# Four of sixteen gates computed by Strassen's scheme inside the values' stage, and queries repeated by transfers

## The chip, the cores and the metric

The kernel runs on one core of one Trainium2 chip. The metric is the device time of one execution in microseconds, the median of several runs. The core has a matrix engine (TensorE, PE in the profile, its weight loads PEld), three other engines that compute (VectorE or DVE, ScalarE or ACT, GpSimd or POOL) and a synchronisation engine (SyncE or SP) that issues most DMA transfers. ACT and POOL issue transfers too, each on a queue of its own. An engine works its instructions off in order.

## The reference

One layer of a decoder trunk on 1024 tokens with 1024 features, in float32:

```python
h    = rms_norm(x, pre_mix_g)
proj = h @ w_in                      # q, k, v of attention A; q, k, v of attention B; 2 x 1024 gates
qa, ka, va, qb, kb, vb, gates = split(proj)
oa   = diff_attention(rope(qa), rope(ka), va, lam)    # 4 heads, two softmaxes of 64-wide queries, v 128 wide
ya   = (rms_norm(oa) * 0.8) @ w_a_out
ob   = merge of three dilated window attentions (4 heads each, 128 wide)
yb   = ob @ w_b_out
g_a, g_b = split(sigmoid(gates))
x    = x + rms_norm((g_a * ya + g_b * yb) @ w_mix_out)
x    = x + rms_norm(conv-gated MLP of rms_norm(x))
```

Attention A is causal; for each of its 4 heads it makes two score matrices (64 features each), takes the softmax of each and subtracts the second, scaled by lambda, from the first. The gates are 2048 columns of the projection, 16 blocks of 128, used only after both attentions.

## The kernel before

A float32 product is made of three matmuls: an operand is split into a high half, rounded to the format that TensorE reads at full speed (`F32R`), and a low half, the rest; `mm3` (L153 to L157) issues high*high, low*high and high*low into one accumulation. `split` (L148) makes the high half by a copy on ACT (L149) and the low half by a subtraction on DVE (L146). A unit of work of TensorE is thus a 128x128 weight and 512 moving columns, three times over.

The work before the convolution stage comes in this order:

1. *The values' stage.* h, not yet divided by its norm, stands in SBUF as `xh` and `xl` (128 features x 8 chunks x 1024 tokens). The 2048 value columns of A and B are computed by Strassen's scheme of seven products (p1 to p7) in two rounds i = 0, 1 of 1024 columns each: feature halves and token halves on the one side (`b11`, `b12`, `b21`, `b22` and the sums `t2`, `t3`, `t4`; `b12` holds the sum T1 until it is made again near the end), column halves on the other. `steps_v` is the hand-written list of 56 steps (product, round, chunk k); a step is 12 matmuls. `fetch_v` loads its weights, one or two 128x512 blocks, 8 to 10 steps ahead into a ring of buffers; `ready_v` adds or subtracts them on DVE (p5, p6, p7, p3) and splits them, 4 steps ahead; `step_v` issues the matmuls, and at the fourth chunk `take_v` moves the sums out of PSUM into quarters of the result. `put_v` scales a quarter by 1/norm and stores it to DRAM from POOL's queue; `STORE_AT` says before which step the first round's quarters are stored. Between steps the list also places the norms (`NORM_AT`), the angles, sines and tables of the rotation (`ANGLES_AT`, `SINES_AT`, `TABLES_AT`) and, from `TABLES_AT + 4` on, more load buffers.
2. *A first gate, and head 0's queries and keys.* `gate(i)` is a projection (`proj_t`): 2 token halves x 8 chunks x 3 matmuls, its weights loaded and split in two pieces by `load_unit`; `put_gate` scales it (L250) and stores it to `gt_d` from ACT's queue.
3. *The first attention (A).* Each of the 4 heads has 8 jobs `attend_a` (128 queries each); PE is given fill between them by `interleave`, in the order of the letters in `A_FILLS`: g is a gate, p the next head's queries and keys (`proj_a`), v, w, x, V fetch or split values, P is the first projection of attention B. Work that follows a job is put off by `later`.
4. *Attention B* with its own fills, and the last three gates (`B_GATES`).

The order in each engine's queue is made by a planner that simulates the traced program with costs of its own; blocks under `high_priority` are moved ahead, and `behind_marks` pins an instruction behind another.

In `proj_a` the rotated queries of one score matrix go into a tile of 128 partitions, high half in one half of the partitions and low half in the other (`q0`, `q1`); the keys' high half is written twice, into both halves of the partitions (`k0`, `k1`, at L756 and L757), and so is their low half (`l0`, `l1`, at L760). One matmul against k and one against l (L783, L784) then give all four terms of the product of 64 features.

PSUM has eight banks: `acc` 3, `pt` 2, `ps_s` 2, `ps_o` 1. In the values' stage a product uses four: p1, p6, p7, p4 three of `acc` and `ps_o`, p2, p5, p3 two of `ps_s` and two of `pt`.

Of the kernel before, what the change touches and what calls it, by code (L numbers as in the profile page):

```python
# [24 lines left out]
P = 128  # L25
# [24 lines left out]
START_GATES, A_FILLS, B_GATES = 1, ("gpgg", "gpvgg", "wgpgg", "xgPVgg"), 3  # L50
# [4 lines left out]
XT_BUFS, NORM_AT, ANGLES_AT, SINES_AT, TABLES_AT, STORE_AT = 6, 14, 25, 33, 34, {35: 0, 36: 3, 39: 2, 41: 1}  # L55
# [32 lines left out]
def trunk(ctx: ExitStack, tc: tile.TileContext, a, out):  # L88
# [111 lines left out]
    def halves():  # L200
        return [slice(i * 512, (i + 1) * 512) for i in range(2)]
# [139 lines left out]
    def f32(v):  # L341
        return v.bitcast(F32)
# [4 lines left out]
    def slot(name, shape=(P, S), dt=F32R):  # L347

        return slots.tile(list(shape), dt, tag="slot", name=name, bufs=SLOTS)
# [111 lines left out]
    with ExitStack() as st_y:  # L461
# [6 lines left out]
        def turns(pattern, *ps):  # L468

            ks = [iter(range(4)) for _ in ps]  # L470
            return [(ps[c], 1, next(ks[c])) for c in pattern]

        steps_v += [("p1", 1, k) for k in range(4)] + turns((0, 0, 1, 0, 1, 0, 1, 1), "p5", "p6")
# [15 lines left out]

        def fetch_v(n):  # L490
            p, i, k = steps_v[n]
            which = {"p1": ((0, 0),), "p2": ((0, 1),), "p5": ((1, 0), (1, 1)), "p6": ((0, 0),), "p7": ((0, 0), (1, 0)),
                     "p4": ((1, 1),), "p3": ((0, 1),)}[p]
            got_v[n] = [load_raw(a["w_v"][j * 4 + k][:, (2 * i + c) * 512 : (2 * i + c + 1) * 512], next(tags), parts=1 if n else 2)
                        for c, j in which]
# [59 lines left out]

        def step_v(n):
            p, i, k = steps_v[n]
            x = xs_of[p]
# [73 lines left out]
        for n in range(8, len(steps_v)):  # L632
# [23 lines left out]
            if n == TABLES_AT:  # L656
                turn_norms()
            if k == 0 and (p, i) in places_y:
                q, name, pool = places_y[p, i]
                quarter[q, i] = new_y(name, pool)  # L660
# [81 lines left out]
    def proj_a(h, res):  # L742
        q0, q1, k0, k1, l0, l1 = (slot(n) for n in ("q0", "q1", "k0", "k1", "l0", "l1"))
        res += [q0, q1, k0, k1, l0, l1]

        def put_q(half, sl, ps):
            t = rotated(ps, cos_a, sin_a, sl, 32)
            nc.scalar.activation(q0[u, sl], t[u], AF.Copy)
            nc.scalar.activation(q1[v, sl], t[v], AF.Copy)
            nc.vector.tensor_tensor(q0[v, sl], t[u], q0[u, sl].bitcast(F32), op=ALU.subtract)  # L750
            nc.vector.tensor_tensor(q1[u, sl], t[v], q1[v, sl].bitcast(F32), op=ALU.subtract)

        def put_k(half, sl, ps):
            t = rotated(ps, cos_a, sin_a, sl, 32)
            for part, kk in ((u, k0), (v, k1)):
                nc.scalar.activation(kk[u, sl], t[part], AF.Copy)  # L756
                nc.scalar.activation(kk[v, sl], t[part], AF.Copy)  # L757
            for part, kk, ll in ((u, k0, l0), (v, k1, l1)):
                for to in (u, v):
                    nc.vector.tensor_tensor(ll[to, sl], t[part], kk[part, sl].bitcast(F32), op=ALU.subtract)  # L760

        yield from proj_t(QA + h * P, put_q)
        yield from proj_t(KA + h * P, put_k)

    def attend_a(h, i, ops, vs, out_sb, pair):

        q0, q1, k0, k1, l0, l1 = ops
# [10 lines left out]
        for c, (qq, kk, ll) in enumerate(((q0, k0, l0), (q1, k1, l1))):  # L778
            s_sb = wk_a.tile([P, S], F32, tag="s", name="s", bufs=4)
            sc.append(s_sb)  # L780
            for n, (c0, c1) in enumerate(chunks):
                ps = psum(F32, ps_s, "s")[:, : c1 - c0]
                nc.tensor.matmul(ps, qq[:, qs], kk[:, c0:c1], start=True, stop=False)  # L783
                nc.tensor.matmul(ps, qq[:, qs], ll[:, c0:c1], start=False, stop=True)  # L784
# [86 lines left out]
    free_gates = list(range(2 * KC))  # L871
# [929 lines left out]
```

## Time and profile before

| | |
|---|---|
| median of three runs | 1688.93 us (1688.74 to 1690.08) |
| the profiled execution | 1693.0 us, its span 1691.1 us |
| granted TensorE clock, mean | 0.997 |
| PE, DVE, ACT, POOL busy | 1672.0, 1318.6, 923.9, 161.9 us |
| values' stage, first gate, head 0's projections | about 5 to 161, 161 to 172, 172 to 194 us |
| first attention with its fills | within 192 to 545 us |
| moved by DMA | 237.40 MB, 140 GB/s |

The profile is of one execution. Busy time of PE counts each matmul to its modelled end, and matmuls overlap, so a busy PE is not yet a PE without gaps; who waited for whom is a view of its own. In a row of a group stand line, engine, operation, what it writes and reads, shape and count, then busy us and mean ns of one, then the engine's idle time just before and what ended it. In a view of stages stand the stage's bounds and length, the busy us (and instructions) of PE, PEld, DVE, ACT and POOL, the granted clock, the busy share of the DMA engines and GB/s.

### The profile page before, as it was taken

What the parts mean: (1) busy time and instruction counts of PE and PEld (TensorE: products, weight loads), DVE (VectorE), ACT (ScalarE), POOL (GpSimd) and SP (SyncE); (2) the same over time, 40 slices, a digit from 0 to 9 for tenths busy, and PEclk for the clock granted to TensorE, in tenths of its full rate; (3) what the DMA queues carried; (4) which work ended last, traced back from release to release, by engine and by line L of the source; (5) the groups of instructions that cost most, each with busy time, mean ns of one, the idle gap of its engine ahead of it and who ended that gap; (6) DMA issues with size and microseconds to landing.
All of it is one profiled execution on the core that took longest, in us unless ns stands there. A gap on an engine that the chain in (4) does not pass through costs nothing. (4 is left out here: it accounts for less than half of the span.)

```text
span 1691.1 us, 22909 instructions
## 1 busy us (share of the span) xinstructions
PE 1672.0 (99%) x7878; PEld 1395.7 (83%) x7878; DVE 1318.6 (78%) x2446; ACT 923.9 (55%) x1723; POOL 161.9 (10%) x251
## 2 busy tenths in 40 slices
PE   9999999999999999999999999999999999999997
PEld 7888888888888888888878888888888888878886
DVE  8794686877777777788866865988888778689978
ACT  7643575655554777667653533565555455255463
POOL 0031000000000000010123400022211121000000
PEclk9999999999999999999999999999999999999999
DMA  8777311214112122333676632267655655296524
GB/s 273 228 248 245 98 59 61 88 57 121 48 63 81 55 72 77 107 120 119 208 257 215 203 112 87 51 162 171 163 132 133 154 134 128 98 338 214 197 88 149
DMA packets 115973, 237.40 MB, mean 140 GB/s; under 512 B 14272, under 2 KB 23424, under 8 KB 115856
## 3 DMA queue, kind: packets, MB, share of 16 engines
q1 hardware_dynamic: 89296, 171.28, 30.4%
q0 software_dynamic: 21808, 56.26, 14.2%
q10 hardware_dynamic: 4752, 8.39, 1.3%
q8 instruction: 62, 1.02, 0.2%
q14 instruction: 55, 0.45, 0.1%
HBM read 177.54 MB, written 47.86 MB: 133 GB/s over the span
## 5 line engine op out<-in xcount | busy, mean ns | idle before, releaser
L157 PE MATMUL acc<-xl,whi 128*128 128x512 f32 x768 | 303.2, 395 | 0.0
L155 PE MATMUL acc<-xh,whi 128*128 128x512 f32 x768 | 302.1, 393 | 0.0
L156 PE MATMUL acc<-xh,wlo 128*128 128x512 f32 x768 | 301.9, 393 | 0.0
L149 ACT ACTIVATE whi<-raw 128x512 fp32r<-128x512 f32 (+1 forms) x249 | 153.9, 626 | 162.6 <-PE acc L157 94.2
L146 DVE TENSOR_TENSOR wlo<-raw,whi 128x512 fp32r<-128x512 f32 (+1 forms) x249 | 171.9, 698 | 27.8 <-ACT whi L149 23.5
L156 PEld LDWEIGHTS acc<-xh,wlo 128*128 128x128 f32 x768 | 144.6, 188 | 28.2
L157 PEld LDWEIGHTS acc<-xl,whi 128*128 128x128 f32 x768 | 144.6, 188 | 28.0
L155 PEld LDWEIGHTS acc<-xh,whi 128*128 128x128 f32 x768 | 144.7, 188 | 27.5
L155 PE MATMUL acc<-mh,whi 128*128 128x512 f32 x384 | 149.7, 390 | 1.4 <-ACT u L1446 1.1
L156 PE MATMUL acc<-mh,wlo 128*128 128x512 f32 x384 | 149.4, 389 | 0.0
L157 PE MATMUL acc<-ml,whi 128*128 128x512 f32 x384 | 149.1, 389 | 0.0
L700 ACT ACTIVATE t<-acc 64x512 f32<-64x512 f32 (+1 forms) x160 | 94.6, 591 | 60.1 <-PE acc L157 58.2
L149 ACT ACTIVATE whi<-s 128x512 fp32r<-128x512 f32 x80 | 49.8, 627 | 90.8 <-PE acc L157 68.7
L1442 DVE TENSOR_TENSOR u<-acc,u 128x512 f32<-128x512 f32 x100 | 68.4, 685 | 28.4 <-PE acc L157 28.2
L701 DVE TENSOR_TENSOR t<-acc,cos 128x512 f32<-128x512 f32 x64 | 44.2, 690 | 59.4 <-ACT t L700 58.9
L155 PEld LDWEIGHTS acc<-mh,whi 128*128 128x128 f32 x384 | 72.1, 188 | 17.4 <-ACT u L1446 2.0
L157 PEld LDWEIGHTS acc<-ml,whi 128*128 128x128 f32 x384 | 72.1, 188 | 15.0
L156 PEld LDWEIGHTS acc<-mh,wlo 128*128 128x128 f32 x384 | 72.1, 188 | 14.7
L1619 PE MATMUL acc<-whi,wlo 128*128 128x512 f32 x216 | 76.0, 390 | 0.0
L1618 PE MATMUL acc<-whi 128*128 128x512 f32 x216 | 74.9, 390 | 0.3 <-ACT whi L149 0.3
L1620 PE MATMUL acc<-wlo,whi 128*128 128x512 f32 x216 | 71.6, 390 | 0.0
L793 ACT ACTIVATE s<-s,mx 128x896 f32<-128x896 f32 (+7 forms) x64 | 49.3, 771 | 35.1 <-DVE mx L786 18.8
(403 smaller groups left out, 4033.9 us busy)
## 6 DMA issues: line engine op xcount, KB each, us to landing
raw<-in_w_in SPq DMA_DIRECT2D x96, 256.0 KB, 2.9
raw<-in_w_v SPq DMA_DIRECT2D x71, 256.0 KB, 5.0
raw<-in_w_up SPq DMA_DIRECT2D x68, 256.0 KB, 3.5
raw<-c_d SPq DMA_DIRECT2D x48, 256.0 KB, 3.7
c_d<-c SPq DMA_DIRECT2D x22, 512.0 KB, 3.9
s<-in_w_up POOLq DMA_DIRECT2D x40, 256.0 KB, 4.1
s<-s POOLq DMA_DIRECT2D x40, 256.0 KB, 3.9
raw<-in_w_down SPq DMA_DIRECT2D x37, 256.0 KB, 3.6
```

What stands on the lines that cost most here:

```text
L146: eng.tensor_tensor(lo, src, hi.bitcast(F32), op=ALU.subtract)
L149: copy = nc.scalar.activation(hi, src, AF.Copy)
L155: nc.tensor.matmul(o, sh, mh, start=first, stop=False, skip_group_check=on)
L156: nc.tensor.matmul(o, sl, mh, start=False, stop=False, skip_group_check=on)
L157: nc.tensor.matmul(o, sh, ml, start=False, stop=last, skip_group_check=on)
L700: nc.scalar.activation(t1[dst], ps[src], AF.Copy)
L701: nc.vector.tensor_tensor(t2, ps, cos[:, sl], op=ALU.mult)
L793: exp = nc.scalar.activation(sc[c][:, :w], sc[c][:, :w], AF.Exp, bias=mx[:, c, 0:1], scale=-1.0, accum_out=den[:, c : c + 1])
L1442: nc.vector.tensor_tensor(to, made(p), x, op=ALU.add)
L1618: nc.tensor.matmul(banks[m], gh[:, tk], wh, start=f == 0, stop=False)
L1619: nc.tensor.matmul(banks[m], gl[:, tk], wh, start=False, stop=False)
L1620: nc.tensor.matmul(banks[m], gh[:, tk], wl, start=False, stop=f == NH - 1)
```

## The change

Four gates, 12 to 15 (`PAIRS` = 2 pairs), are no longer computed by `gate`; `A_FILLS` has two letters g for each head where there were three. They become 14 new steps of the values' stage, in place behind the fourth chunk of p1 in round 1, at step 36: for each of p2, p1, p5, p6, p7, p4, p3 one step for either pair, again of 12 matmuls (4 chunks, one 512-column output). Here the gates' weights are stationary and h moves. A pair has a bank of `pt` and one of `ps_s`, accumulated across products as the values' are, while the values' p1 rests in its four banks. `fetch_v` loads the blocks from `w_in`; `ready_v` is unchanged. `take_gate` moves a product out, scales it by 1/norm and stores it from POOL's queue. The results stand in the tiles of the values' first and third quarters ("a0", "b3") between their uses; the stores of the first round's quarters are moved to steps 32, 37, 42 and 46.

In `proj_a` the keys' tile now holds the high half in one half of the partitions and the low half in the other, each written once, and the queries are repeated instead: high halves (`a0`, `a1`) and low halves (`b0`, `b1`) are computed for one half of the partitions and copied to the other by four transfers a head from POOL's queue, behind the second token half. The number and shape of the matmuls of the scores stay.

```diff
-START_GATES, A_FILLS, B_GATES = 1, ("gpgg", "gpvgg", "wgpgg", "xgPVgg"), 3
+PAIRS, START_GATES, A_FILLS, B_GATES = 2, 1, ("gpg", "gpvg", "wgpg", "xgPVg"), 3
-... TABLES_AT, STORE_AT = ..., 34, {35: 0, 36: 3, 39: 2, 41: 1}
+... TABLES_AT, STORE_AT = ..., 34, {32: 0, 37: 3, 42: 2, 46: 1}
-        steps_v += [("p1", 1, k) for k in range(4)] + turns((0, 0, 1, 0, 1, 0, 1, 1), "p5", "p6")
+        steps_v += [("p1", 1, k) for k in range(4)]
+        steps_v += [(p, "gate", x) for p in ("p2", "p1", "p5", "p6", "p7", "p4", "p3") for x in range(PAIRS)]
+        steps_v += turns((0, 0, 1, 0, 1, 0, 1, 1), "p5", "p6")
...
+            if i == "gate":
+                srcs = [w_in[where[GT + gate_of(k, c) * P]][:, j * 512 : (j + 1) * 512] for c, j in which]
...
+        def take_gate(p, n, use):
+            def put(q):
+                sl = halves()[q % 2]
+                y = gate_y[n][q]
+                tt(y, use if p == "p4" else y, rstd_row[:, sl], ALU.mult)
+                nc.gpsimd.dma_start(gt_d[gate_of(n, q // 2)][:, sl], y)
+            y = gate_y[n]
+            if p in ("p2", "p6", "p7"):
+                nc.scalar.activation(y[{"p2": 0, "p6": 1, "p7": 3}[p]], use, AF.Copy)
+            if p == "p1":
+                tt(y[0], use, y[0], ALU.add)
+                put(0)
+            if p == "p7":
+                tt(y[3], banks[n, False], y[3], ALU.add)
+                put(3)
+            if p == "p4":
+                put(2)
+            if p == "p3":
+                tt(y[1], use, y[1], ALU.add)
+                put(1)
+        def step_gate(p, n, wh, wl):
+            left = p in ("p1", "p6", "p7", "p4")
+            if p in ("p1", "p2"):
+                banks[n, left] = psum(F32, pt, "pt") if left else psum(F32, ps_s, "s")
+            x, use = xs_of[p], banks[n, left]
+            for k in range(4):
+                c = slice(k * P, (k + 1) * P)
+                mm3(use, wh[:, c], wl[:, c], x[0][:, k], x[1][:, k], k == 0 and p in ("p1", "p2", "p5"), k == 3, p in ("p6", "p7", "p4", "p3"))
+            with tc.high_priority(offset=80):
+                take_gate(p, n, use)
...
+            if (p, i, k) == ("p2", "gate", 0):
+                ya, yb = new_y("a0"), new_y("b3", yw)
+                gate_y.update({x: {0: ya[x], 1: ya[2 + x], 3: yb[x], 2: yb[2 + x]} for x in range(PAIRS)})
...
         def put_q(half, sl, ps):
             t = rotated(ps, cos_a, sin_a, sl, 32)
-            nc.scalar.activation(q0[u, sl], t[u], AF.Copy)
-            nc.scalar.activation(q1[v, sl], t[v], AF.Copy)
-            nc.vector.tensor_tensor(q0[v, sl], t[u], q0[u, sl].bitcast(F32), op=ALU.subtract)
-            nc.vector.tensor_tensor(q1[u, sl], t[v], q1[v, sl].bitcast(F32), op=ALU.subtract)
+            for part, hi in ((u, a0), (v, a1)):
+                nc.scalar.activation(hi[part, sl], t[part], AF.Copy)
+            for part, hi, lo in ((u, a0, b0), (v, a1, b1)):
+                nc.vector.tensor_tensor(lo[part, sl], t[part], f32(hi[part, sl]), op=ALU.subtract)
+            if half:
+                for x, from_, to in ((a0, u, v), (a1, v, u), (b0, u, v), (b1, v, u)):
+                    side(x[to], x[from_])
         def put_k(half, sl, ps):
             t = rotated(ps, cos_a, sin_a, sl, 32)
             for part, kk in ((u, k0), (v, k1)):
-                nc.scalar.activation(kk[u, sl], t[part], AF.Copy)
-                nc.scalar.activation(kk[v, sl], t[part], AF.Copy)
-            for part, kk, ll in ((u, k0, l0), (v, k1, l1)):
-                for to in (u, v):
-                    nc.vector.tensor_tensor(ll[to, sl], t[part], kk[part, sl].bitcast(F32), op=ALU.subtract)
+                nc.scalar.activation(kk[part, sl], t[part], AF.Copy)
+            for part, to, kk in ((u, v, k0), (v, u, k1)):
+                nc.vector.tensor_tensor(kk[to, sl], t[part], f32(kk[part, sl]), op=ALU.subtract)
...
-    free_gates = list(range(2 * KC))
+    free_gates = list(range(2 * (KC - PAIRS)))
```

More of the change, by code (lines that the diff above doesn't have):

```diff
@@ L49 @@
 MIX_UNITS = {3: (0,), 4: (1,), 5: (2, 4), 6: (5,), 7: (6, 3, 7)}
-START_GATES, A_FILLS, B_GATES = 1, ("gpgg", "gpvgg", "wgpgg", "xgPVgg"), 3
+PAIRS, START_GATES, A_FILLS, B_GATES = 2, 1, ("gpg", "gpvg", "wgpg", "xgPVg"), 3
 SLOTS = 18
 LEFT_PAD = 48
-XT_BUFS, NORM_AT, ANGLES_AT, SINES_AT, TABLES_AT, STORE_AT = 6, 14, 25, 33, 34, {35: 0, 36: 3, 39: 2, 41: 1}
+XT_BUFS, NORM_AT, ANGLES_AT, SINES_AT, TABLES_AT, STORE_AT = 6, 14, 25, 33, 34, {32: 0, 37: 3, 42: 2, 46: 1}
 K_FIRST = (4, 0, 5, 1, 6, 2, 7, 3)
@@ L488, in new_y, with gate_of @@
             return [(pool or yv).tile([P, 512], F32, tag=f"y{name}{m}", name="yv") for m in range(4)]
+        def gate_of(x, c):
+            return 2 * (KC - PAIRS + x) + c
         def fetch_v(n):
@@ L493, in fetch_v @@
                      "p4": ((1, 1),), "p3": ((0, 1),)}[p]
-            got_v[n] = [load_raw(a["w_v"][j * 4 + k][:, (2 * i + c) * 512 : (2 * i + c + 1) * 512], next(tags), parts=1 if n else 2)
-                        for c, j in which]
+            if i == "gate":
+                srcs = [w_in[where[GT + gate_of(k, c) * P]][:, j * 512 : (j + 1) * 512] for c, j in which]
+            else:
+                srcs = [a["w_v"][j * 4 + k][:, (2 * i + c) * 512 : (2 * i + c + 1) * 512] for c, j in which]
+            got_v[n] = [load_raw(src, next(tags), parts=1 if n else 2) for src in srcs]
         def ready_v(n, w=512):
@@ L554, in trunk @@
         banks = {}
+        gate_y = {}
+        def take_gate(p, n, use):
[28 more added lines that the diff above has]
+                take_gate(p, n, use)
         def step_v(n):
             p, i, k = steps_v[n]
+            if i == "gate":
+                step_gate(p, k, *ready.pop(n))
+                return
             x = xs_of[p]
@@ L742, in proj_a @@
     def proj_a(h, res):
-        q0, q1, k0, k1, l0, l1 = (slot(n) for n in ("q0", "q1", "k0", "k1", "l0", "l1"))
-        res += [q0, q1, k0, k1, l0, l1]
+        a0, a1, b0, b1, k0, k1 = (slot(n) for n in ("a0", "a1", "b0", "b1", "k0", "k1"))
+        res += [a0, a1, b0, b1, k0, k1]
         def put_q(half, sl, ps):
             t = rotated(ps, cos_a, sin_a, sl, 32)
-            nc.scalar.activation(q0[u, sl], t[u], AF.Copy)
-            nc.scalar.activation(q1[v, sl], t[v], AF.Copy)
-            nc.vector.tensor_tensor(q0[v, sl], t[u], q0[u, sl].bitcast(F32), op=ALU.subtract)
-            nc.vector.tensor_tensor(q1[u, sl], t[v], q1[v, sl].bitcast(F32), op=ALU.subtract)
+            for part, hi in ((u, a0), (v, a1)):
[5 more added lines that the diff above has]
+                    side(x[to], x[from_])
         def put_k(half, sl, ps):
@@ L765, in attend_a @@
     def attend_a(h, i, ops, vs, out_sb, pair):
-        q0, q1, k0, k1, l0, l1 = ops
+        a0, a1, b0, b1, k0, k1 = ops
         scale = QK ** -0.5
@@ L777, in attend_a @@
         sc = []
-        for c, (qq, kk, ll) in enumerate(((q0, k0, l0), (q1, k1, l1))):
+        for c, (qh, ql, kk) in enumerate(((a0, b0, k0), (a1, b1, k1))):
             s_sb = wk_a.tile([P, S], F32, tag="s", name="s", bufs=4)
@@ L782, in attend_a @@
                 ps = psum(F32, ps_s, "s")[:, : c1 - c0]
-                nc.tensor.matmul(ps, qq[:, qs], kk[:, c0:c1], start=True, stop=False)
-                nc.tensor.matmul(ps, qq[:, qs], ll[:, c0:c1], start=False, stop=True)
+                nc.tensor.matmul(ps, qh[:, qs], kk[:, c0:c1], start=True, stop=False)
+                nc.tensor.matmul(ps, ql[:, qs], kk[:, c0:c1], start=False, stop=True)
                 mask = mask_a[:, 512 - (c1 - c0) :] if c1 == w else mask_a[:, 0:1].to_broadcast([P, 512])
```

## The prediction

> **What bounds the kernel now.** I read the page's busy shares and slices first, then the waits of TensorE (PE), then its timeline, then each engine's busy time by stage.
>
> ```profile
> span 1691.1 us, 22909 instructions
> PE 1672.0 (99%) x7878; PEld 1395.7 (83%) x7878; DVE 1318.6 (78%) x2446; ACT 923.9 (55%) x1723; POOL 161.9 (10%) x251
> PEclk9999999999999999999999999999999999999999
> ```
>
> TensorE is busy for 99% of the span, at full clock nearly everywhere. A busy PE could still hide waits, because the ends of its matmuls are modelled; so the view of PE's waits comes next (what waited, for whom: total us, times, longest).
>
> ```profile
> PE acc L155 <- ACT xh L387: 2.3, 2, 1.4
> PE pt L713 <- ACT rows L1050: 1.4, 1, 1.4
> PE o L725 <- DVE osb L1027: 1.2, 1, 1.2
> PE acc L155 <- DVE ya L1210: 0.8, 1, 0.8
> ```
>
> No wait is longer than 1.4 us, and none of the helpers that feed the projections or the first attention (the splits at L146 and L149, the scores' L786) heads a long one. TensorE's own work is the bound, so a matmul less is time won, at the spacing of matmuls and not at their length. The timeline of PE shows both (start, duration):
>
> ```profile
> 150.44 0.39 PE L155 MATMUL acc<-whi,t4h 128*128 128x512 f32 x1
> ...
> 152.93 0.39 PE L157 MATMUL o<-wlo,t4h 128*128 128x512 f32 x1
> ```
>
> Between these two rows stand ten more matmuls: eleven steps in 2.49 us, 0.226 us each, although each is drawn 0.39 us long.
>
> **The change, part by part.**
>
> *Matmuls.* A gate is a projection of 128 columns: two halves of the tokens, eight chunks, three matmuls each, 48 in all and 10.9 us at 0.226. Four gates are 192 matmuls (43.5 us), all in the first attention now. Strassen's scheme takes two gates as a 2x2 problem with seven products of 4 chunks and three matmuls: 7 x 12 x 2 pairs = 168 matmuls (38.0 us), put behind the values' step 35. PE gains 24 x 0.226 = **5.4 us**. The scores keep their number and shapes of matmuls, so the repeated queries give PE nothing.
>
> The rows above give 0.226 us for a 512-column matmul with a weight load of its own. The Trainium skill, "TensorE: Matmul & The Clock Gate", section Back-to-back issue gap, states that a sustained stream of such pairs with N=512 comes to about 131 ns each. By that figure the 24 matmuls would be worth an estimated 3.1 us, and the forecast would lie near 1686; the trace disagrees with it by the eleven steps above, and the sum goes by the trace.
>
> *What the first attention loses and keeps.* The other engines' rows (busy us, mean ns, idle) and the stages (length, busy time of PE, PEld, DVE, ACT, POOL, clock, DMA) that bear on this:
>
> ```profile
> L250 DVE TENSOR_TENSOR gate<-acc,rstd_row 128x512 f32<-128x512 f32 x32 | 22.0, 688 | 17.1 <-PE acc L157 16.8
> L760 DVE TENSOR_TENSOR l<-t,k 64x512 fp32r<-64x512 f32 x32 | 21.9, 685 | 0.9 <-ACT k L757 0.4
> L757 ACT ACTIVATE k<-t 64x512 fp32r<-64x512 f32 x16 | 10.1, 630 | 0.3
> L146 DVE TENSOR_TENSOR wlo<-raw,whi 128x512 fp32r<-128x512 f32 (+1 forms) x249 | 171.9, 698 | 27.8 <-ACT whi L149 23.5 <-DMA sin<-tab_d 2.7 <-PE acc L156 0.8
> L149 ACT ACTIVATE whi<-raw 128x512 fp32r<-128x512 f32 (+1 forms) x249 | 153.9, 626 | 162.6 <-PE acc L157 94.2 <-issue 15.0 <-PE acc L1619 13.0
> L550 DVE TENSOR_SCALAR yv<-yv,edge 128x512 f32<-128x512 f32 x20 | 8.3, 475 | 0.0
> ```
>
> ```profile
> 78.00:104.00 26.00, 26.00 (x117) 21.52 (x116) 25.83 (x49) 11.93 (x17) 0.00 (x0) 1.00 0.51 158
> 104.00:144.00 40.00, 40.00 (x182) 33.20 (x181) 32.70 (x61) 16.43 (x28) 16.22 (x23) 1.00 0.81 287
> 192.00:545.00 353.00, 353.00 (x1761) 297.63 (x1760) 271.70 (x680) 202.43 (x410) 2.01 (x4) 1.00 0.23 74
> 380.00:400.00 20.00, 20.00 (x99) 16.79 (x99) 19.00 (x46) 16.35 (x30) 0.00 (x0) 1.00 0.54 145
> ```
>
> The gates were what PE ran while the softmax went through VectorE (DVE) and ScalarE (ACT), so their loss thins the cover. The first attention lies in 192 to 545 us. It loses 43.5 of 353 us of PE. DVE loses four gates of two splits (L146) and two scalings (L250) each, 16 x 0.69 = 11.0 us, and the second copy of the keys' low halves: 16 of the 32 instructions at L760, 11.0 us. DVE goes from 271.7/353 = 77% to 249.7/309.5 = 81%. ACT loses 8 splits (5.0 us) and the 16 second copies of the keys' high halves (L757, 10.1 us): 57% to 61%. Locally the worst is a stretch like 380 to 400, where the projections of the next head are rotated: DVE 19.0 of 20 us, and PE waited for nothing. It is there that the keys' 4 instructions a head go, so it gets no denser. I take **0** for thinner cover, with 0 and 2.8 us as bounds: two waits as long as PE's longest above. A gain is excluded, since PE waits for nothing there that lighter engines could shorten.
>
> *The repeated queries.* Four transfers a head on POOL's queue, 16 in all, 256 KB each, copy one half of the partitions to the other. The nearest rows are the engine's own cost of an issue and the landing times (KB each, median us to landing):
>
> ```profile
> L1408 POOL DMA_DIRECT2D s<-s x40 | 34.9, 872 | 120.1 <-ACT s L1406 67.0 <-ACT whi L149 21.3 <-DVE c L1358 5.6
> raw<-in_w_in SPq DMA_DIRECT2D x96, 256.0 KB, 2.9
> raw<-in_w_v SPq DMA_DIRECT2D x71, 256.0 KB, 5.0
> s<-s POOLq DMA_DIRECT2D x40, 256.0 KB, 3.9
> v_d<-yv POOLq DMA_DIRECT2D x32, 256.0 KB, 5.1
> gt_d<-gate ACTq DMA_DIRECT2D x32, 256.0 KB, 2.2
> ```
>
> Four issues of 0.87 us and a landing of 3.9 us make 7.4 us behind the second half of the queries. The keys' projection follows at once with 48 matmuls, 10.9 us, and its own rotation; the scores need both, and the keys come last. POOL is busy 2 of 353 us there. Cost **0**; if that cover were gone, up to 7.4 us at the first head alone, since later heads have a whole gate behind their projections.
>
> *The values' stage gains 14 steps.* Loads on SP's queue: 18 of 256 KB in place of 8 (products with a difference of weights load two). ACT: 14 splits and 6 copies, 20 x 0.63 = 12.6 us in 38 us. POOL: 8 stores of gates that were issued by ACT; nobody waits for them until much later, but the values' stores stand behind them. The stage 104 to 144 us moves 287 GB/s; the 26 transfers of 256 KB are 6.8 MB in 38 us more, 179 GB/s. That leaves DVE: 14 low halves, 8 sums of weights, 6 additions and 8 scalings, 36 instructions. Its timeline at the tightest split of this stage, and PE's first matmul that uses that split:
>
> ```profile
> 120.52 0.68 DVE L345 TENSOR_TENSOR raw<-raw 128x512 f32<-128x512 f32 x1
> 121.12 0.68 DVE L146 TENSOR_TENSOR wlo<-wz,whi 128x512 fp32r<-128x512 f32 x1
> ```
>
> ```profile
> 123.24 0.39 PE L155 MATMUL acc<-whi,t2h 128*128 128x512 f32 x1
> ```
>
> DVE's starts lie 0.60 us apart, so the 36 take 21.6 us. In the 38 us of the new steps stand these, less the 6 that are prepared up to five steps before them (3.6), plus the 10 that the next five value steps want ahead (6.0), the 16 scalings of the first half's quarters (L550, 6.6), 6 for the tables and 4 additions (6.0): 36.6 us, 96%. Just before, from 78 to 104 us, it was 25.8 of 26. So cover counts: the split above ended at 121.80, 1.4 us before its use, the smallest margin of the steps behind 36. The first four new steps need no sums of weights, which lightens the load just there. I take **0**, bounds 0 and 4.9 us (a wait with its half clock, below).
>
> *Banks.* The new steps accumulate in two banks each of the pools of L713's and the scores' tiles. The value step behind them (p5) starts in the bank that the last gate step has just filled, so its second output tile waits for one DVE addition, with three matmuls (0.68 us) as cover. The nearest row is L155 waiting for DVE ya, 0.8 us; I take **0.4**, bounds 0 and 1.2 (the row of DVE osb).
>
> The sum: 5.4 - 0.4 = 5.0 us. The profiled execution took 1693.0 us (span 1691.1 and 1.9 around it), the median of the runs is 1688.93, 4.1 lower; the sum is taken from either, and the median gives **1683.9 us**. A change under 0.2%, 3.4 us here, is what a measurement can't tell from none: faster begins below 1685.6, slower above 1692.3.
>
> **Rivals.**
>
> *One late wait and the half clock.* A short stretch of this trace shows what a wait can cost beyond itself:
>
> ```profile
> 570.00:572.00 2.00, 1.28 (x9) 0.91 (x7) 0.18 (x1) 2.00 (x7) 0.00 (x0) 1.00 0.00 0
> 572.00:574.00 2.00, 1.23 (x7) 0.95 (x8) 2.00 (x4) 2.00 (x5) 0.00 (x0) 1.00 0.02 4
> 574.00:576.00 2.00, 2.00 (x13) 1.96 (x11) 2.00 (x6) 2.00 (x5) 0.00 (x0) 0.59 0.02 4
> 576.00:578.00 2.00, 1.43 (x7) 1.28 (x7) 2.00 (x4) 1.30 (x5) 0.00 (x0) 0.50 0.00 0
> 578.00:580.00 2.00, 2.00 (x9) 1.90 (x9) 2.00 (x4) 0.03 (x1) 0.00 (x0) 0.50 0.60 238
> 580.00:582.00 2.00, 2.00 (x8) 1.54 (x7) 2.00 (x7) 1.98 (x3) 0.00 (x0) 0.71 0.11 37
> ```
>
> PE idled 0.72 + 0.77 = 1.5 us, and then the granted clock was about 0.5: the shares missing in these rows, (0.41 + 0.50 + 0.50 + 0.29) x 2 us, are 3.4 us. A new wait of 1.5 us, in the dense DVE of the new steps, would cost 4.9 us and leave 1688.4: no change. The margin of 1.4 us speaks for it, the 5-step lead of the weights against it. Chance 0.13. The Trainium skill, "TensorE: Matmul & The Clock Gate", Part 1: The HAM clock gate, puts the drop behind an idle window of about 3.4 us. By that rule such a wait would cost only its own 1.5 us, and the change would still be faster; the rows above disagree, with 1.5 us.
>
> *DVE falls behind in the new steps (the other side).* 96% holds only if nothing is queued badly. Low halves that come 1.5 us late at two steps cost 2 x 4.9 = 9.8 us: 1693.3, slower. It decides from the second such wait on. For it: 25.8 of 26 us just before; against it: no wait at all in the values' dense stretch now. Chance 0.09.
>
> *The freed tiles come late.* The gates' first results go into the tiles of the first quarter, which must be stored first. Its factor is known only about here (PE, DVE and POOL in their timelines):
>
> ```profile
> 105.99 0.39 PE L155 MATMUL pt<-whi,xh 128*128 128x512 f32 x1
> ...
> 108.49 1.04 PE L434 MATMUL s<-ident,rstd_row 128*128 128x128 f32 x8
> ```
>
> ```profile
> 104.19 4.83 DVE L550 TENSOR_SCALAR yv<-yv,edge 128x512 f32<-128x512 f32 x12
> ```
>
> ```profile
> 105.07 7.27 POOL L551 DMA_DIRECT2D v_d<-yv  x7 [34.55 <-DVE yv L550]
> ```
>
> The first step behind step 35 starts with the first of these rows, at 106.0, with the transposes of the norms (1.0 us) inside it or the next. ACT's copy of the first product, at about 109 us, waits for a store; behind it on ACT's queue stand the weights' splits. The fourth store is issued near 109.2 and lands 5.1 later, 114.3; the bank is wanted at 106 + 4 steps x 2.7 + 1 = 118. If the store were the last of the seven (112.3 + 5.1 = 117.4) it would still do; two us beyond that PE waits some 1.5 us with the half clock, 1688.4. Chance 0.03.
>
> *The first attention becomes DVE's.* If the thinner cover costs its bound of 2.8 us, 1686.7: no change. 81% against it. Chance 0.05.
>
> *More than the matmuls.* The 4.1 us between profile and median suggest that the timed runs lack the half clock. If they have it, and the new timing removes it: 1683.9 - 3.4 = 1680.5. Chance 0.05.
>
> **How the numbers follow.** The forecast, 1683.9 (own range 1683.5 to 1685.5), has 0.65. Faster: 0.65 + 0.05 = 0.70. No change: 0.13 + 0.03 + 0.05 = 0.21. Slower: 0.09. The range reaches from the best case, 1680.5, to the single wait at 1688.4 with some play: 1680.3 to 1688.8; it leaves out the slower case and little else.
>
> **What would show it.** Right: 24 fewer matmuls at a spacing of 0.226; no new row over 1 us among PE's waits; 192 to 545 shorter by 43.5 us, the values' stage longer by 38 to 38.5; L760 and the keys' ACT copies halved; the transfers landing before the keys' low halves. Wrong: a PE wait on whi or wlo in 106 to 150 us, a wait on the queries' transfers, a window below clock 1.0 in the values' stage, or DVE above 90% over the whole first attention.

## The result, and the profile after

The changed kernel takes **1705.74 us** (median of four runs, 1702.2 to 1709.02), the kernel before on the same chip 1689.36 us (1688.74 to 1690.08): a ratio of 1.0096, 95% interval 1.0083 to 1.0108. It is slower, by 16 us, where 5 us less were forecast; the time lies far above the range.

The page of the changed kernel first:

```profile
span 1700.1 us, 22950 instructions
PE 1672.2 (98%) x7854; PEld 1395.5 (82%) x7854; DVE 1319.4 (78%) x2450; ACT 921.0 (54%) x1719; POOL 171.5 (10%) x275
```

The 24 matmuls are gone (7878 before), and yet the span is 9.0 us longer. By busy shares nothing has happened. The view of PE's waits (what waited, for whom: total us, times, longest) tells more:

```profile
PE s L835 <- DVE mx L838: 4.2, 3, 3.1
PE acc L155 <- DVE t L752: 3.8, 1, 3.8
PE acc L155 <- DVE ya L1262: 3.4, 3, 1.5
PE pt L764 <- ACT rows L1102: 1.7, 1, 1.7
```

Before, no wait was longer than 1.4 us. The first two rows are new, and both lie in the first attention: the scores (L835) wait for the row maxima that DVE takes from the scores before them (L838, the line L786 of before), and the projections wait for a bank that DVE's rotation (L752) frees. The same stretches in the view by stage of the changed kernel (length; busy us of PE, PEld, DVE, ACT, POOL; granted clock; DMA):

```profile
104.00:142.00 38.00, 38.00 (x173) 31.55 (x172) 32.97 (x58) 11.37 (x20) 12.56 (x23) 1.00 1.02 372
142.00:199.00 57.00, 57.00 (x253) 47.18 (x253) 31.13 (x48) 22.31 (x37) 6.32 (x12) 1.00 0.42 135
230.00:545.00 315.00, 305.56 (x1512) 256.47 (x1511) 239.62 (x623) 182.93 (x379) 6.79 (x13) 0.98 0.27 81
402.00:417.00 15.00, 9.79 (x34) 7.04 (x33) 14.56 (x37) 8.81 (x17) 2.06 (x4) 0.77 0.47 112
526.00:545.00 19.00, 14.77 (x70) 12.18 (x69) 16.66 (x46) 12.57 (x25) 0.00 (x0) 0.82 0.22 70
580.00:600.00 20.00, 17.49 (x97) 14.98 (x96) 18.05 (x43) 16.59 (x40) 0.00 (x0) 0.91 0.15 48
```

and the one such stretch of the kernel before:

```profile
570.00:590.00 20.00, 17.93 (x91) 15.36 (x90) 17.61 (x39) 16.04 (x38) 0.00 (x0) 0.83 0.14 44
```

The values' stage with its 14 new steps (first two rows) has no gap and full clock. The time is lost in three short stretches. PE idles 5.2, 4.2 and 2.5 us there, and the clock takes the missing share of 15, 19 and 20 us: 3.5, 3.4 and 1.8 us. That is 20.6 us; before, the third stretch alone existed and cost 2.1 + 3.4 = 5.5. The difference, 15.1, less 5.4 for the 24 matmuls, is 9.7, and the spans differ by 9.0: between the two profiled executions the account closes within 0.7 us. (PE's waits outside these stretches are 1.0 us shorter in all than before.)

The timed medians differ by 16.4. The profiled execution was the fastest of the four, at a mean clock of 0.993; the others, 2.6 to 6.8 us slower, had 0.991 to 0.992, which is at most 1.7 to 3.4 us more lost to the clock (0.001 of the time for each 0.001; it is at most that, since a mean clock also counts half clock behind the last matmuls, where it costs nothing); the rest of it no trace shows. The kernel before has the half clock in some of its executions and in others not: of its 17 later runs the seven with a clock of 0.999 took 1687.17 to 1689.37, the three with 0.995 or 0.996 took 1691.82 to 1692.84, and its profiled execution had 0.997.

What PE waits for in the first new stretch, in the timeline of the changed kernel (start, duration, idle before and releaser in brackets), cut to what bears on the wait:

```profile
402.39 0.69 DVE L838 CUSTOM_DVE_ANT_0 s<-s,mask_a 128x512 f32<-128x512 f32 x1
...
403.00 1.22 DVE L146 TENSOR_TENSOR vl<-vperm,vh 128x1024 fp32r<-128x1024 f32 x1
405.21 1.22 DVE L146 TENSOR_TENSOR vl<-vperm,vh 128x1024 fp32r<-128x1024 f32 x1
...
406.35 0.68 DVE L838 CUSTOM_DVE_ANT_0 s<-s,mask_a 128x512 f32<-128x512 f32 x1
...
406.96 2.83 DVE L802 TENSOR_TENSOR b<-t,a 64x512 fp32r<-64x512 f32 x4
...
407.43 0.40 PE L836 MATMUL s<-k,b 128*128 128x512 f32 x1
...
410.16 0.68 DVE L838 CUSTOM_DVE_ANT_0 s<-s,mask_a 128x512 f32<-128x512 f32 x1
...
410.91 0.47 PE L835 MATMUL s<-k,a 128*128 128x128 f32 x1 [3.08 <-DVE mx L838]
```

DVE is busy for 14.56 of these 15 us, and none of its instructions is slow. They run in the order of its queue: splits of values (1.22 us each) and the four low halves of the next head's queries (L802, 2.83) stand ahead of the reductions that would free the scores' banks. Before, such a queue stood in the same head and cost nothing. The timeline of the kernel before, cut in the same way:

```profile
379.10 0.69 DVE L786 CUSTOM_DVE_ANT_0 s<-s,mask_a 128x512 f32<-128x512 f32 x1
...
380.27 0.39 PE L157 MATMUL acc<-xl,whi 128*128 128x512 f32 x1
...
381.03 0.68 DVE L750 TENSOR_TENSOR q<-t,q 64x512 fp32r<-64x512 f32 x1
...
381.94 0.69 DVE L751 TENSOR_TENSOR q<-t,q 64x512 fp32r<-64x512 f32 x1
382.08 0.39 PE L157 MATMUL acc<-xl,whi 128*128 128x512 f32 x1
...
383.87 0.68 DVE L786 CUSTOM_DVE_ANT_0 s<-s,mask_a 128x512 f32<-128x512 f32 x1
```

Here the two reductions start 4.8 us apart, more than the 3.8 us in the changed kernel (406.35 and 410.16), and PE runs 18 matmuls of projections between them. Between 402.2 and 413.6 us the changed kernel's timeline has not one. The second stretch is at the end of the last head, with the same kind of queue. There PE's next matmul is itself one of a projection, but its bank waits for a rotation (L752) in that queue:

```profile
531.15 0.39 PE L778 MATMUL o<-pt,vl 128*128 128x128 f32 x2
...
531.79 1.22 DVE L146 TENSOR_TENSOR vl<-vperm,vh 128x1024 fp32r<-128x1024 f32 x1
...
533.33 1.29 DVE L947 TENSOR_TENSOR ql<-t,qh 128x512 fp32r<-128x512 f32 x2
...
534.61 1.28 DVE L752 TENSOR_TENSOR t<-acc,cos 128x512 f32<-128x512 f32 x2
535.34 0.79 PE L155 MATMUL acc<-xh,whi 128*128 128x512 f32 x1 [3.80 <-DVE t L752]
```

### The profile page after: what moved, and what is told of

Read it like the earlier page. It is cut to its first block, busy times and chain, and to the rows that moved or that the text cites. A ratio compares the mean times of both kernels' runs of the same rounds, so it can differ in the third digit from the quotient of the medians.

```text
span 1700.1 us, 22950 instructions
## 1 busy us (share of the span) xinstructions
PE 1672.2 (98%) x7854; PEld 1395.5 (82%) x7854; DVE 1319.4 (78%) x2450; ACT 921.0 (54%) x1719; POOL 171.5 (10%) x275
## 5 line engine op out<-in xcount | busy, mean ns | idle before, releaser
L155 PE MATMUL acc<-xh,whi 128*128 128x512 f32 x704 | 278.6, 396 | 3.8 <-DVE t L752 3.8
L156 PE MATMUL acc<-xh,wlo 128*128 128x512 f32 x704 | 278.3, 395 | 0.0
L157 PE MATMUL acc<-xl,whi 128*128 128x512 f32 x704 | 278.0, 395 | 0.0
L155 PEld LDWEIGHTS acc<-xh,whi 128*128 128x128 f32 x704 | 133.3, 189 | 30.0 <-DVE t L752 4.0
L156 PEld LDWEIGHTS acc<-xh,wlo 128*128 128x128 f32 x704 | 133.3, 189 | 26.0
L157 PEld LDWEIGHTS acc<-xl,whi 128*128 128x128 f32 x704 | 133.1, 189 | 25.8
L752 DVE TENSOR_TENSOR t<-acc,cos 128x512 f32<-128x512 f32 x64 | 44.0, 690 | 55.3 <-ACT t L751 54.7
L838 DVE CUSTOM_DVE_ANT_0 s<-s,mask_a 128x512 f32<-128x512 f32 (+3 forms) x96 | 51.9, 552 | 20.0 <-PE s L836 12.5
```

What stands on the lines that cost most here:

```text
L155: nc.tensor.matmul(o, sh, mh, start=first, stop=False, skip_group_check=on)
L156: nc.tensor.matmul(o, sl, mh, start=False, stop=False, skip_group_check=on)
L157: nc.tensor.matmul(o, sh, ml, start=False, stop=last, skip_group_check=on)
L752: nc.vector.tensor_tensor(t2, ps, cos[:, sl], op=ALU.mult)
L838: nc.vector.tensor_tensor_reduce(out=s_sb[:, c0:c1], in0=ps, in1=mask, scale=-scale, scalar=3.0e38, op0=ALU.add, op1=ALU.min, accum_out=mx ...
```

## The experiments

Two theories stood at first: that the gates were the cover of the first attention, so that their loss costs time whatever the values' stage does; and that the cost comes from the other half, the queries with their transfers. A third, for the queries alone, was that the planner's order makes waits that nobody can place. Later ones are about which head needs the cover, and are told where they come up. Each ratio is to the kernel before on the same chip.

| run | median us (range) | ratio to before, 95% interval |
|---|---|---|
| changed kernel | 1705.74 (1702.2 to 1709.02) | 1.0096, 1.0083 to 1.0108 |
| gates only | 1711.1 (1707.75 to 1711.62) | 1.0118, 1.0103 to 1.0133 |
| queries only | 1685.77 (1685.09 to 1688.99) | 0.9975, 0.9965 to 0.9984 |
| one pair | 1706.76 (1705.66 to 1710.23) | 1.01, 1.0085 to 1.0115 |
| cover again | 1732.6 (1731.79 to 1732.88) | 1.0248, 1.0231 to 1.0265 |
| cover for heads 0, 1 | 1714.08 (1713.56 to 1715.76) | 1.0145, 1.0128 to 1.0162 |
| cover for heads 2, 3 | 1720.4 (1719.56 to 1720.83) | 1.018, 1.0165 to 1.0195 |
| cover from B | 1701.67 (1699.88 to 1702.89) | 1.0069, 1.0054 to 1.0084 |
| one pair, full cover in A | 1704.16 (1702.92 to 1706.35) | 1.0086, 1.0071 to 1.0101 |
| gates first | 1736.32 (1734.96 to 1738.48) | 1.0279, 1.026 to 1.0299 |
| jobs first | 1695.78 (1690.98 to 1698.3) | 1.0035, 1.0022 to 1.0048 |
| queries only, jobs first | 1682.57 (1681.65 to 1683.83) | 0.9956, 0.9945 to 0.9968 |
| gates late, jobs first | 1687.75 (1685.4 to 1690.8) | 0.999, 0.9981 to 0.9998 |

### The two halves of the change

*Gates only:* the changed kernel with the queries, keys and scores of before.

```diff
-            for x, from_, to in ((a0, u, v), (a1, v, u), (b0, u, v), (b1, v, u)):
-                side(x[to], x[from_])
...
+            for part, kk, ll in ((u, k0, l0), (v, k1, l1)):
+                for to in (u, v):
+                    nc.vector.tensor_tensor(ll[to, sl], t[part], kk[part, sl].bitcast(F32), op=ALU.subtract)
```

> The gates' 14 steps are kept, queries and keys are made as in the kernel before. Theory COVER (with a third of its gates gone, the first attention has too little fill, PE waits for DVE's mask reductions and each long wait brings a half clock): the waits stay, 1698 to 1712 us, two or more stretches of half clock between 390 and 545 us. Theory QUERIES (the repeated queries cost the time: four copies in a row on ACT and four subtractions in a row on DVE, then transfers, hold the reductions back): the waits in the first attention go, about 1684 us.

*Queries only:* no pair of gates in the values' stage, three gates a head, the stores where they were.

```diff
-PAIRS, START_GATES, A_FILLS, B_GATES = 2, 1, ("gpg", "gpvg", "wgpg", "xgPVg"), 3
+PAIRS, START_GATES, A_FILLS, B_GATES = 0, 1, ("gpgg", "gpvgg", "wgpgg", "xgPVgg"), 3
...
```

> No gate is moved; only queries and keys are made as after the change. COVER: no new wait, 1689 us as before or up to 1 us less. QUERIES: PE waits of 3 us for DVE's reductions near the end of a query projection, 1697 us or more. A third theory, ORDER (the planner's order of the engines' queues happens to put PE's scores ahead of the fill at some places, whatever was changed): a wait may come at places that nobody can name, 1686 to 1700 us.

The halves add up: 1.0118 x 0.9975 = 1.0093, against 1.0096 for both. The gates cost 20 us, as the first theory had it. The queries gain 4, more than any theory had. In the view by stage, the two new stretches are there with the gates alone, the first of them worse (6.3 us idle, 6.8 to the clock), the second not (3.9 and 1.7):

```profile
402.00:422.00 20.00, 13.68 (x44) 9.67 (x44) 18.97 (x48) 13.44 (x25) 0.00 (x0) 0.66 0.21 58
535.00:545.00 10.00, 6.08 (x22) 4.76 (x22) 9.77 (x24) 5.36 (x10) 0.00 (x0) 0.83 0.15 48
```

With the queries alone they aren't, and the stretch behind the first attention, where before lost 5.5 us, is whole:

```profile
556.00:576.00 20.00, 20.00 (x107) 17.18 (x106) 16.64 (x34) 15.59 (x32) 0.00 (x0) 1.00 0.28 88
```

The gain of the queries is not the half clock alone: the runs with a clock of 0.999 are 1685.34 to 1687.36 here (five, median 1685.77) and 1688.23 to 1689.22 for before, measured together with them (three). Between the two profiled executions it is the stretch at 570 us: PE's idle time falls from 19.1 to 16.9 us and the 3.4 us of clock go, 5.6 in all, and the spans differ by 5.6 (1691.1 and 1685.5).

### How much of it is cover

*Cover again:* the changed kernel, and the first attention computes the four gates a second time, as before. 192 matmuls, 43.5 us, are thus done twice.

```diff
-PAIRS, START_GATES, A_FILLS, B_GATES = 2, 1, ("gpg", "gpvg", "wgpg", "xgPVg"), 3
+PAIRS, START_GATES, A_FILLS, B_GATES = 2, 1, ("gpgg", "gpvgg", "wgpgg", "xgPVgg"), 3
...
-    free_gates = list(range(2 * (KC - PAIRS)))
+    free_gates = list(range(2 * KC))
```

> The changed kernel, with the four gates computed a second time as fill of the first attention (three gates a head): 192 matmuls more, 43.5 us. COVER: the waits and half clocks of the first attention go, so it is not 1705.7 + 43.5 = 1749 but about 1684 + 43.5 = 1727.5 us. QUERIES: they stay, 1740 us or more.

```profile
390.00:550.00 160.00, 160.00 (x822) 135.66 (x821) 120.83 (x327) 83.61 (x178) 2.06 (x4) 1.00 0.27 80
```

This stretch of the view by stage takes in both places of waits, and none is left. 1732.6 less the 43.5 us of repeated work is 1689.1: 16.6 us of the changed kernel's time are the missing cover (18 by the ratios of the table, as the kernel before was 1.4 us slower beside this run). The time is 5 us above the 1727.5 that the first theory expected. Nor is 1689.1 the 1679.7 that the parts would give (1683.9, less 4.2 for the queries): waits of 1 to 2.8 us in other stages and one stretch at half clock have come in their place. By the profiles these are 5.7 us of idle time and 1.7 of clock more than with the queries only. Added to that kernel's 1685.5, with 43.5 for the repeated work and less 5.4 for the 24 matmuls, they give 1731.0; the span is 1731.1.

*One pair:* two gates in the values' stage, three in heads 2 and 3.

```diff
+PAIRS, START_GATES, A_FILLS, B_GATES = 1, 1, ("gpg", "gpvg", "wgpgg", "xgPVgg"), 3
```

> One pair of gates moved (7 steps), heads 0 and 1 with two gates, heads 2 and 3 with three as before; queries as after the change. COVER: heads 2 and 3 have their cover again, where both long waits lay: about 1689.4 - 2.7 = 1686.7 us. QUERIES: the wait at the query projection during head 2 stays, 1692 us or more.

Half of the gates moved costs as much as all, 20 us more than the first theory had. The wait at the end of head 3 is gone, that of head 2 stands unchanged, and a new one has come into the values' stage, by the view of waits:

```profile
PE pt L155 <- DVE yv L345: 3.6, 1, 3.6
```

With one pair, the next product comes after one step and not two, so DVE's addition has half the cover; that this is the cause was not tested apart. With smaller waits beside it PE idles 5.7 us there (110 to 134 us), and the clock takes 3.4 more. This run changed two things at once, so heads and pairs were taken apart next.

### Which head needs it

That head 2 waits although heads 2 and 3 have their three gates back, gave two theories. *Local:* a head needs its own three gates. *Drawn ahead:* heads 0 and 1 take three gates' worth whatever they are given, and the shortage is carried on. In two runs two of the gates are computed a second time (96 matmuls, 21.7 us), for heads 0 and 1 (shown), or for heads 2 and 3 (`('gpg', 'gpvg', 'wgpgg', 'xgPVgg')`). The expectations below call the second theory STOCK.

```diff
-PAIRS, START_GATES, A_FILLS, B_GATES = 2, 1, ("gpg", "gpvg", "wgpg", "xgPVg"), 3
+PAIRS, START_GATES, A_FILLS, B_GATES = 2, 1, ('gpgg', 'gpvgg', 'wgpg', 'xgPVg'), 3
...
-    free_gates = list(range(2 * (KC - PAIRS)))
+    free_gates = list(range(2 * (KC - PAIRS) + 2))
```

> The changed kernel with two gates computed a second time, as third gates of heads 0 and 1 only (96 matmuls, 21.7 us). Theory STOCK (fill is drawn ahead of its head whenever the attention's chain of reduction, exponential and sum is not ready, so what is missing anywhere shows at the end of the attention): the wait behind the last head stays, the one in head 2 goes, about 1705.7 + 21.7 - 8 = 1719 us. Theory LOCAL (a head waits when its own fill is too little): heads 2 and 3 keep both waits, 1727 us.

> The same two gates a second time, as third gates of heads 2 and 3 only (21.7 us). LOCAL: both waits go, 1684 to 1689 + 21.7 = 1706 to 1711 us. STOCK: the wait at the end gets shorter and the one in head 2 stays, as in the kernel with one pair: 1714 to 1720 us.

By stage, head 2 with cover for heads 0 and 1:

```profile
402.00:417.00 15.00, 15.00 (x71) 12.46 (x70) 13.56 (x29) 11.27 (x20) 0.00 (x0) 1.00 0.10 37
```

and head 2 and the end of head 3 with cover for heads 2 and 3:

```profile
402.00:420.00 18.00, 12.80 (x44) 9.46 (x43) 17.20 (x42) 10.84 (x21) 2.06 (x4) 0.72 0.58 147
526.00:545.00 19.00, 19.00 (x105) 16.34 (x104) 15.46 (x42) 11.48 (x24) 0.00 (x0) 1.00 0.26 84
```

Gates given to heads 0 and 1 free head 2; gates given to head 2 itself don't. Net of the repeated 21.7 us the first takes 1692.4 and the second 1698.7, so the cover of heads 0 and 1 is worth 13.3 us and that of heads 2 and 3 7.0 (together more than the 16.6 of both: they don't simply add). *Local* falls. *Drawn ahead* had one thing wrong: with cover for heads 0 and 1 it expected the wait at the end of the last head to stay, and some 1719 us. That wait is gone too, and only the stretch just behind the first attention (578 to 604 us) idles more, 4.5 us against the changed kernel's 2.5. A count supports the drawing ahead: the projections' matmuls that PE has run in the timeline when a head's first score matmul starts (from the first attention's first fill on), less what the heads so far were given (48 for a gate, 96 for the next head's queries and keys).

| drawn ahead at the start of | head 1 | head 2 | head 3 | the end | waits in the first attention |
|---|---|---|---|---|---|
| before | 69 | 60 | 65 | 29 | none |
| changed | 89 | 132 | 113 | 120 | head 2, the end |
| cover for heads 0, 1 | 41 | 32 | 77 | 104 | none |
| cover for heads 2, 3 | 89 | 132 | 60 | 30 | head 2 |
| jobs first (below) | 90 | 108 | 122 | 120 | head 2, the end |
| gates late, jobs first (below) | 90 | 108 | 69 | 44 | head 2 |

Heads 0 and 1 of the changed kernel run 240 and 235 such matmuls where 192 each are given to them. The rest is taken from the fill of the heads behind. The runs left out fit: gates only has 114, 168, 136 and 120 and waits in head 2 and at the end, one pair 89, 132, 60 and 30 and waits in head 2, and four with three gates in every head (queries only, cover again, and the next two) 41, 32, 29 and -10 and no wait. Why a head takes that much, and what limit makes one wait, isn't settled: 113 and 122 at the start of head 3 passed without a wait in head 3 before its end.

### Where else the cover could come from

*Cover from B:* nothing is computed twice; the first gate and the three of attention B fill the first attention.

```diff
+PAIRS, START_GATES, A_FILLS, B_GATES = 2, 0, ("gpgg", "gpvgg", "wgpgg", "xgPVgg"), 0
```

> Both pairs by Strassen's scheme, and all other twelve gates in the first attention, three a head: none before it and none at the end of the second attention (B_GATES 0). If the cover is all that the change lacks, and the end of the second attention needs none: about 1681 us. If every stage needs its cover: no wait in the first attention, new waits of some 10 to 20 us in all where the three gates of the second attention stood, 1690 to 1705 us.

*One pair, full cover in A:* two gates in the values' stage, and two of attention B's three fill the first attention.

```diff
+PAIRS, START_GATES, A_FILLS, B_GATES = 1, 1, ("gpgg", "gpvgg", "wgpgg", "xgPVgg"), 1
```

> One pair by Strassen's scheme (12 matmuls less, 2.7 us), three gates in each head of the first attention, one before it and one at the end of the second (in place of three). COVER: no wait in the first attention; the wait of one pair's p6 for p1's addition in the values' stage stays (3.8 us and a half clock): about 1685.8 - 2.7 + 7 = 1690 us, more if the second attention lacks its two gates.

The waits of the first, then of the second:

```profile
PE acc L155 <- ACT oah L149: 2.9, 2, 1.9
PE o L776 <- DVE osb L1079: 2.8, 1, 2.8
PE acc L155 <- ACT obh L149: 2.8, 1, 2.8
```

```profile
PE acc L155 <- ACT oah L149: 4.4, 1, 4.4
PE acc L155 <- ACT obh L149: 3.9, 1, 3.9
```

The first attention has none in either. The waits have gone to 840 to 938 us, where B's gates had stood, with half clock behind them; the second also idles 4.9 us in the values' stage (112 to 130 us), at full clock. B's three gates were thus in use as cover, and moving the hole moves the waits. The first gate was not: with none ahead of the first attention, the first of the two runs has no wait over 0.6 us from 130 to 830 us.

*Gates first:* nine gates ahead of the first attention and none in it, to see how long a head is without any. Two theories: a head's own chain of score, softmax and product keeps it at 72 to 76 us; or DVE's work does, at some 55 us a head.

```diff
+PAIRS, START_GATES, A_FILLS, B_GATES = 2, 9, ("p", "pv", "wp", "xPV"), 3
```

> The changed kernel with the eight gates of the first attention taken out of it and put ahead of it (START_GATES 9): the same work, but the heads have only the projections as fill. Theory CHAIN (a head of the first attention takes some 72 to 76 us whatever fill it has, because its reductions, exponentials and sums follow one another across DVE and ACT; PE's matmuls only fill the time): the heads stay near 70 us each, PE waits in all of them, 1705.7 + 60 to 90 us. Theory BUSY (a head takes as long as its busiest engine, and DVE has some 55 us of work a head): heads of 55 to 58 us, 1706 to 1730 us.

Heads 1, 2 and 3 by stage:

```profile
390.70:446.30 55.60, 49.56 (x239) 41.24 (x237) 46.18 (x142) 34.86 (x80) 0.10 (x1) 0.89 0.22 64
446.30:504.20 57.90, 50.98 (x244) 40.34 (x244) 50.19 (x142) 35.51 (x78) 2.07 (x4) 0.88 0.25 73
504.20:558.40 54.20, 48.73 (x244) 39.94 (x243) 44.36 (x138) 29.36 (x72) 0.00 (x0) 0.94 0.09 30
```

No chain keeps a head at 72 us: they take 54 to 58. But DVE is busy for 44 to 50 of these, so its load alone isn't the length either, and the total is the worst of all, beyond what the second theory allowed. PE idles 5.5 to 7 us a head, in waits of at most 1.9 us each, and 3 to 7 us more go to the clock.

### The order alone

*Jobs first:* the changed kernel; the planner puts the jobs of both attentions further ahead of the fill (`jobs` serves both). No work is added or removed.

```diff
         for i, fn in enumerate(todo):
-            with tc.high_priority(offset=30):
+            with tc.high_priority(offset=100):
```

> The changed kernel, the attention's jobs marked as more urgent in the planner (high_priority offset 100 in place of 30). If the chain of a head is long because reductions stand behind the rotations on DVE: shorter heads, under 70 us, the waits in head 2 and at the end shrink, 1690 to 1698 us. If the planner's order is hardly moved by it: within 4 us of 1705.7.

```profile
402.00:412.00 10.00, 7.70 (x35) 5.83 (x35) 8.94 (x20) 5.16 (x9) 2.07 (x4) 1.00 1.08 241
524.00:534.00 10.00, 6.39 (x22) 5.04 (x23) 9.73 (x24) 5.24 (x10) 0.00 (x0) 0.83 0.16 53
574.00:582.00 8.00, 5.45 (x30) 4.57 (x27) 6.58 (x16) 7.30 (x18) 0.00 (x0) 0.79 0.00 1
```

10 us less by order alone. The three places are still there; at the first one PE now idles 2.3 us in place of 5.2 and the clock stays at 1.00. Not all of the gain is in the first attention: the changed kernel idles 4.1 us between 860 and 920 us, at attention B's end and in the output projection behind it, and this one not at all there. The heads hardly get shorter (71.9, 70.1 and 72.2 us from one first score matmul to the next, 71.8, 76.3 and 70.1 before the new order).

*Gates late, jobs first:* that order, and the short rations at heads 0 and 1 (two gates) and not at heads 2 and 3 (three), paid for by the first gate and one of B's.

```diff
+PAIRS, START_GATES, A_FILLS, B_GATES = 2, 0, ("gpg", "gpvg", "wgpgg", "xgPVgg"), 2
+            with tc.high_priority(offset=100):
```

> The changed kernel with the jobs placed 100 ahead, no gate ahead of the first attention, two gates in heads 0 and 1, three in heads 2 and 3, and two left for attention B (in place of one, two in each, and three). The theory that heads 0 and 1 draw on the fill of the later ones: what is given late is still there at heads 2 and 3, so no wait in the second half of the first attention, and the waits of the first half are those of 1 to 2 us under this order: 1686 to 1692, that is the 1685.8 of the queries alone, less 5.4 for the 24 matmuls, plus one or two waits with their half clock (4 to 5 us each). The rival, that a head needs its own three gates: heads 0 and 1 show the waits that heads 2 and 3 showed, 1695 to 1702.

*Queries only, jobs first:* the better half alone, with that order.

```diff
+PAIRS, START_GATES, A_FILLS, B_GATES = 0, 1, ("gpgg", "gpvgg", "wgpgg", "xgPVgg"), 3
+            with tc.high_priority(offset=100):
```

> The kernel before with the queries' half of the change alone (all sixteen gates as projections, three to a head), and the attention's jobs placed 100 ahead in the planner's order in place of 30. The order by itself gave the changed kernel 10 us, where fill was short. If the gain of that order lies in the sharing out of a cover that is too thin, there is little to gain here, where the cover is whole: 1685.8 as without the new order, within 1683 to 1688. If the order is better by itself, whatever the cover, it gives several us here too: 1676 to 1681.

Gates late gives 1687.75, within what the drawing ahead had: the wait at the end is gone, two stretches remain, by stage

```profile
393.00:402.00 9.00, 6.71 (x25) 4.90 (x24) 7.72 (x21) 4.19 (x9) 1.83 (x4) 0.81 1.04 232
580.00:592.00 12.00, 9.61 (x48) 8.32 (x47) 10.78 (x26) 8.48 (x19) 0.00 (x0) 0.72 0.20 61
```

of 2.3 + 1.7 and 2.4 + 3.4 us. Queries only with the same order takes 1682.57, measured together with it, and by its waits PE has next to none in either attention:

```profile
PE acc L155 <- ACT xh L387: 1.4, 1, 1.4
PE pt L642 <- DVE t4l L639: 1.2, 1, 1.2
```

(L387 and L642 are in the first 30 us.) That is 0.4 us below what the first theory allowed and 1.6 above the second; against queries only in the old order the intervals of the ratios just touch, so from the times alone the order's own gain here, some 3 us, is not certain. The profiles show where it comes from: of the queries-only kernel's waits

```profile
PE acc L155 <- DVE ya L1262: 3.1, 2, 2.8
```

is the largest; PE idles 4.1 us between 848 and 898 us, and with the new order not at all there. So the order is worth something where no gate is missing too. This is the best kernel of all, 0.9956 of before, without a single gate moved. At its order the four gates by Strassen's scheme, with 24 matmuls less and the best sharing found, cost 5.2 us: the two stretches, 9.8 us, less 5.4 are 4.4 of it.

## Why the prediction was wrong, step by step

- *Matmuls:* right. There are 24 fewer; the values' stage ends 38 us later (199 us against 161); the spacing of 0.226 us held, as the account above closes with 5.4.
- *The values' stage:* right in its cost. 36 instructions more on DVE, and no wait from 104 to 199 us. The transfers were not spread out as estimated (179 GB/s): they crowd into 104 to 142 us with 372 GB/s, and PE waits for none of them. Neither "DVE falls behind in the new steps" nor "the freed tiles come late" took place, and the 0.4 us for the banks was not there to see.
- *What the first attention loses and keeps:* **this step failed.** It was sized at 0, with 2.8 us as bound, and measured 16.6 us by the run with cover again. It went wrong in two places. The first is the measure: it reasoned from DVE's share of the attention, 77% before and 81% after. Measured, the share fell, to 239.62 of 315 us (76%), and PE waited all the same, for a queue that is served in order, for 3 us at a time. What counts is whether PE has a matmul that needs none of the queued work, not how busy DVE is on average. The second is the place: the stretch 380 to 400 us with DVE at 19 of 20 us was read as proof that a dense DVE doesn't hurt. It was dense and free of waits while PE had projections to run, 72 of its 99 matmuls there, the next head's and a gate's; it showed the cover at work. That the cover is drawn ahead, so that head 2 pays for heads 0 and 1, was not in the reckoning at all.
- *The bound* of 2.8 us came from the longest waits of a kernel that had the cover. The wait that takes its place could not be seen in those rows.
- *Queries:* costed at 0, which missed a gain of 4 us. Their transfers land in 3.2 and 4.4 us, and PE waits nowhere for them, as expected. The step on the cover had excluded a gain with "PE waits for nothing there that lighter engines could shorten"; the wait just behind the first attention, at 571 us, stood in the rows shown, and with the queries alone it went away. The rival "More than the matmuls" had named its half clock, at 0.05.
- *The rivals:* "The first attention becomes DVE's" had the place and a chance of 0.05, and its sign to look for, DVE above 90%, would have missed it. None of the signs listed as wrong appeared; among those listed as right, "no new row over 1 us among PE's waits" failed. "One late wait and the half clock" had the price of one wait: 4.9 us from before's stretch, 8.7 and 7.6 from the two that came. It looked for the wait in the new steps. The case that happened is both together, two new waits of which each drags the clock down, and neither rival had that sum. The chance of 0.09 for slower stood for a cause in the new steps that did not occur.

What stays open: what the planner's order does by itself and what it does by sharing out the cover is not fully apart, since it also took waits away where no gate was missing. The changed kernel's other runs are up to 6.8 us slower than the profiled one. Their mean clock explains at most 1.7 to 3.4 us of it; which waits stand behind the rest isn't known.

## What to carry to other kernels

Independent matmuls between the steps of a softmax are not work to be made cheap elsewhere: before moving them, count how many of them stand in PE's order between the dependent steps, here head by head, and find what queue PE would wait for without them. A mean busy share can't show that, and a stretch without waits says nothing on what happens without its cover. Here cover was drawn ahead from a common stock by a planned order, so the hole opened behind the heads that it was taken from, and a change of that order was worth more than the work saved (10 us against 5.4).

## What the runs showed of the hardware

A wait's length didn't set whether the clock dropped. With queries only, PE idles 2.79 us in one piece near 895 us and keeps full clock (by stage):

```profile
894.00:898.00 4.00, 1.21 (x7) 0.67 (x5) 3.02 (x4) 0.00 (x0) 0.76 (x1) 1.00 0.00 1
898.00:902.00 4.00, 4.00 (x18) 3.31 (x19) 3.90 (x7) 0.63 (x1) 1.73 (x4) 1.00 0.85 273
```

With jobs first, 2.3 us of idling in 402 to 412 us cost no clock; with gates late, 2.3 us in 393 to 402 and 2.4 in 580 to 592 did, and before's 1.5 us at 571 too. The stretches at half clock (twice the time that the clock takes in the rows by stage) are 3.4, 6.8, 10.2 (cover for heads 2, 3) or 13.7 us long (gates only, 402 to 422 us). The Trainium skill, "TensorE: Matmul & The Clock Gate", Part 1: The HAM clock gate, describes a window of 3413 ns that runs freely, whatever the kernel does. The lengths agree with it, multiples of 3.4 us, and so would the accidental drops, if it depends on how a wait falls into the window; no run here tests that. Its condition, an idle window, doesn't agree: 1.5 us of idling was enough. In these runs, stretches with 1.5 to 4.5 us of idling cost 0 to 3.4 us of clock besides, and those with 4.9 to 6.3 us cost 0 (one pair, full cover in A, 112 to 130 us) to 6.8 (gates only).
